# Softmax times values in plain float32, two heads side by side in TensorE's columns

## The chip, the core and the metric

The kernel runs on one core of one Trainium2 chip. The metric is device microseconds of the whole program: a median of 1966.94 over three runs (1965.1 to 1971.12). Engines are named as in the profile: PE is the matrix engine's matmuls, PEld its weight loads, DVE the vector engine, ACT the scalar engine, SP the queue that issues the DMAs. TensorE is granted its full 2.4 GHz in nearly the whole run (mean 0.996 of it).

## The reference, cut to what matters

Two transformer layers (MLA attention, neighbourhood attention, gated merge, MLP) run on 256 latent and 256 context tokens, then an mLSTM mixer and a windowed attention with a sink. In every attention, probabilities meet values:

```python
p = jax.nn.softmax(s, axis=-1).astype(v.dtype)
return jnp.einsum("bhqk,bkhe->bqhe", p, v)     # all float32, head dimension e = 64
```

MLA and neighbourhood attention have 8 heads per layer, the last attention 16 query heads. Layer 0 does this for the context tokens (256 keys) and the latent ones (512 keys), layer 1 and the last attention for the latent ones alone.

## The kernel before

Everything is computed with features or tokens on 128 partitions. Float32 products are made in three matmuls of the one-pass type `float32r`: each operand is stored as a rounded high part and a remainder (`split`, lines 728 to 734: ACT casts the high part, DVE subtracts to get the low one), and `mm3` (736) adds high·high, high·low and low·high. The class `HL` (663) holds such pairs.

An attention works by pairs of heads. `softmax_t` (1079) takes the scores of 128 queries in PSUM, makes the probabilities, transposes them on PE in blocks of 128 into PSUM, and splits the result into `pt`: one tile per head, with high and low part, up to 4 blocks of keys (`kt` = 4, or 2 for context queries) and 256 queries. `pv_mm` (1128) then multiplies values and `pt`: the values are the stationary operand, 256 queries stream. For head 1 of the pair the stationary operand is 128 columns wide (the 64 columns left of the head's come along), so its result lies in PSUM rows 64 to 127; head 0 then overwrites rows 0 to 63 with 64 columns. For `kt` = 4 that is 2 heads x 4 blocks x 3 = 24 matmuls, for `kt` = 2 it is 12. The values are split too: `vt0` and `vt` for neighbourhood attention, `mv` for MLA, `vt` and `v0` in `attn`. There are 32 such products: 16 in layer 0 (8 pairs, `kt` 2 and 4), 8 in layer 1, 8 in the last attention.

`pair_scores` (1111) is the place that already shares the array: two heads' scores contract over 64 rows each, in its upper and lower half, in turn, as one group.

All engine instructions are recorded first. `Recorder.flush` (336) then lists them by a planner with an own cost for each operation (`cost`, 287), 20 passes, free of the order in which the code is written; the lists are the engines' program order. `group` and `close` (184 to 201) make of several matmuls one operation that nothing is put between; its cost is the sum of the matmuls' times a share, plus 0.1. `either` lets the planner choose between ACT and DVE for one operation. Work of all stages shares 16 buffers of the tag `s8` (weights, `HL` pairs, `pt`). DVE also carries a background product over the modulation weights (`junk`), ACT and DVE split each weight chunk (`w`).

Of the kernel before, what the change touches and what calls it, by code (L numbers as in the profile page):

```python
# [6 lines left out]
F32 = mybir.dt.float32  # L7
# [127 lines left out]
class Recorder:  # L135
# [53 lines left out]
    def close(self):  # L189
        op, calls = self.open, self.calls  # L190
        self.open = None

        def run():
            for fn, a, k in calls:
                r = fn(*a, **k)  # L195
            return r

        op.fn, op.a, op.k = run, (), {}
        op.dur = op.dur * self.share + 0.1
        op.deps.discard(op.idx)  # L200
        self.ops.append(op)
# [472 lines left out]
class Kernel:  # L674
# [403 lines left out]

    def softmax_t(self, score, nk, pt, q0, bias=None, sink=None):

        nc, v = self.nc, self.nc.vector
        if callable(score):
            s = self.psum("S")
            p = self.t2()
            nc.hold(p)
            score(s[:, :nk])
        else:
            s, p = score
        if bias is not None:
            v.tensor_tensor(s[:, bias[0]], s[:, bias[0]], bias[1], ALU.add)  # L1090
        nm, ss = self.small(1), self.small(1)
        v.tensor_reduce(nm, s[:, :nk], AX.X, ALU.max, negate=True)
        if sink is not None:
            v.tensor_tensor(nm, nm, sink[0], ALU.min)
        nc.scalar.activation(p[:, :nk], s[:, :nk], AF.Exp, bias=nm, accum_out=ss)
        if sink is not None:
            es = self.small(1)
            nc.scalar.activation(es, nm, AF.Exp, bias=sink[1])
            v.tensor_tensor(ss, ss, es, ALU.add)
        v.reciprocal(ss, ss)  # L1100
        nc.either(lambda e: e.vector.tensor_scalar(p[:, :nk], p[:, :nk], ss, None, ALU.mult),
                  lambda e: e.scalar.activation(p[:, :nk], p[:, :nk], AF.Copy, scale=ss))
        tp = self.psum("T")
        nc.hold(pt)
        kt = nk // P
        for k in range(kt):
            nc.tensor.transpose(tp[:, k * P:(k + 1) * P], p[:, k * P:(k + 1) * P], self.cs("ident"))
        tv = tp[:, :nk].rearrange("p (k q) -> p k q", k=kt)
        self.split(tv, pt[:, 0, :kt, q0:q0 + P], pt[:, 1, :kt, q0:q0 + P])

# [14 lines left out]
    def new_pt(self):  # L1125
        return self.sb.tile([P, 2, 4, 256], F32R, tag="s8", name="pt")

    def pv_mm(self, ps, vt, vcols, pts, kt, first=None):


        def lhs(wh, k, e):
            c0, c1 = vcols
            if e == 0:
                return vt.ap(wh, k, slice(c0, c0 + 64))
            if c1 + k + wh == 0:
                return first
            f = (wh * vt.per + k) * vt.width + c1
            return vt.t[0].rearrange("p a k c -> p (a k c)")[:, f - 64:f + 64]

        for e in (1, 0):  # L1140
            for k in range(kt):
                self.mm3(ps[:128 if e else 64, :256], tuple(lhs(wh, k, e) for wh in (0, 1)),
                         (pts[e][:, 0, k, :], pts[e][:, 1, k, :]), k == 0, k == kt - 1)


    def block1(self, l, x, streams):
# [50 lines left out]
        kr = self.sb.tile([P, 4, 32], F32, tag="kr", name="kr")  # L1197
        vt0 = HL(self, 4, 256, per=4)

        def consume_v(j, ps):  # L1200
            self.split(ps[:, :256], vt0.ap(0, j), vt0.ap(1, j))
            nc.scalar.copy(kr[:, j], ps[:, 256:])
# [4 lines left out]
        nc.sync.dma_start(self.rw, self.i["rw"][l:l + 1].to_broadcast([P, NRW]))  # L1207
        qa, ka, mv = [], [], []
        for hf in range(2):
            ka_ = self.sb.tile([P, 4, 4, 96], F32, tag="tm", name="tm")  # L1210
            mv_ = HL(self, 4, 256, per=4)

            def consume_kv(j, ps, ka_=ka_, mv_=mv_):
                pv = ps.rearrange("p (h e) -> p h e", h=4)
                nc.scalar.activation(ka_[:, j, :, 0:64], pv[:, :, 0:64], AF.Copy, scale=rk[:, j:j + 1])
                hi = mv_.ap(0, j).rearrange("p (h e) -> p h e", h=4)
                lo = mv_.ap(1, j).rearrange("p (h e) -> p h e", h=4)
                self.split_scaled(pv[:, :, 64:128], rk[:, j:j + 1], hi, lo)

# [3 lines left out]
            ka.append(ka_)  # L1223
            mv.append(mv_)
            qa_ = self.sb.tile([P, nq, 4, 96], F32, tag="tm", name="tm")
# [21 lines left out]
        for pair in range(4):  # L1247
            pts = {}
            for e in range(2):
# [11 lines left out]
                for gi, toks, kt, cs in groups:  # L1261
                    pt = pts[gi, e] = self.new_pt()
                    for qi, j in enumerate(toks):
                        qs = slice(toksq.index(j) * P, toksq.index(j) * P + P)

                        def score(s, kt_=kt_, qt_=qt_, qs=qs, kt=kt):
                            n = kt * P
                            self.mm3(s, (qt_[:96, 0, qs], qt_[:96, 1, qs]), (kt_[:96, 0, :n], kt_[:96, 1, :n]),
                                     True, True)

                        self.softmax_t(score, kt * P, pt, qi * P)
            for gi, toks, kt, cs in groups:
                c = pair % 2 * P
                self.head_out(mv[pair // 2], (c, c + 64), [pts[gi, e] for e in range(2)], kt, y_mla, pair, csr(cs))
        if self.stage == 3:
# [5 lines left out]
        na = []  # L1281
        for hf in range(2):
            c0 = OFF_NA + hf * 256
            vt = HL(self, 4, 256, per=4) if hf else vt0
            if hf:
                self.tm_linear2(w_in, 0, c0 + 1024, h, range(4),
                                lambda j, ps, vt=vt: self.split(ps, vt.t[0][:, 0, j:j + 2], vt.t[0][:, 1, j:j + 2]))
            na.append([vt])
        for hf in range(2):
# [7 lines left out]
            rk_, rq_ = (self.tm_rstd(t.rearrange("p j h d -> p (j h) d")) for t in (k_, q_))  # L1297
            na[hf] = (q_, k_, na[hf][0], rq_, rk_)
        self.mark(f"b1.{l}.naat")
        for hf in range(2):  # L1300
            q_, k_, vt, rq_, rk_ = na[hf]
            for pair in range(2):
# [3 lines left out]
                for gi, toks, kt, cs in groups:  # L1306
                    pts = [self.new_pt() for _ in range(2)]
                    for qi, j in enumerate(toks):
                        qo = toksq.index(j) * P
                        sc = self.pair_scores(qt_, kt_, slice(qo, qo + P), kt * P)  # L1310
                        for e in range(2):
                            self.softmax_t(sc[e], kt * P, pts[e], qi * P,
                                           bias=(LAT, biases[e][:, qi, :]) if gi == 1 else None)
                    self.head_out(vt, (pair * P, pair * P + 64), pts, kt, y_na, hf * 2 + pair, csr(cs), True)
        if self.stage == 4:
# [77 lines left out]

    def head_out(self, vt, vcols, pts, kt, y, pair, cs, flip=False):
        ps = self.psum("T")
        self.pv_mm(ps, vt, vcols, pts, kt)
        d = lambda ap: ap.rearrange("p (j q) -> p j q", j=2)
# [338 lines left out]
    def attn(self, x):  # L1736
# [9 lines left out]
        k_ = self.sb.tile([P, 4, 4, 64], F32, tag="tm", name="tm")  # L1746
        vt = HL(self, 4, 256, per=4)
        v0 = self.sb.tile([P, P], F32R, tag="mk", name="v0")
        flat = lambda t: t.rearrange("p h d -> p (h d)")
# [9 lines left out]
        def keys(_):  # L1759
            self.mark(f"at.kv")  # L1760
            self.tm_linear2(w, 0, 1024, h, (2, 3, 0, 1), lambda j, ps: nc.scalar.copy(two(k_, j), ps))
            self.tm_linear2(w, 0, 1280, h, (2, 3, 0, 1),
                            lambda j, ps: self.split(ps, vt.t[0][:, 0, j:j + 2], vt.t[0][:, 1, j:j + 2]))
            nc.scalar.copy(v0.rearrange("p (o d) -> p o d", o=2),
                           vt.ap(0, 0, slice(0, 64)).rearrange("p (o d) -> p o d", o=1).to_broadcast([P, 2, 64]))
            self.tm_rms(k_.rearrange("p j h d -> p (j h) d"), self.rws("at_k"))
# [28 lines left out]
        def heads(hf):  # L1795
# [3 lines left out]
            for pair in range(2):  # L1799
                pts = [self.new_pt() for _ in range(2)]  # L1800
                qt_ = self.paired(q_, range(2), pair, 0.125)
                for qi in range(2):
# [3 lines left out]
                    for e in range(2):  # L1806
                        hd = hf * 4 + pair * 2 + e
                        self.softmax_t(sc[e], 512, pts[e], qi * P, bias=(far, tri),
                                       sink=(nsink[:, hd:hd + 1], sink[:, hd:hd + 1]))
                ps = self.psum("T")  # L1810
                self.pv_mm(ps, vt, (hf * 64, hf * 64), pts, 4, v0)
                m = hf * 2 + pair
# [151 lines left out]
```

## Time and profile before

| | before |
|---|---|
| runs, median (lowest to highest) | 1966.94 us (1965.1 to 1971.12) |
| the profiled execution's own time, its span | 1966.36 us, 1964.6 us |
| PE busy, PEld busy | 1925.8 us (98%), 1701.3 us (87%) |
| DVE busy, ACT busy | 1625.1 us (83%), 931.5 us (47%) |
| chain that ended last | PE 92%, DVE 5%, DMA 2%, ACT 1% |

PE counts as busy from a matmul's start to its modelled end, and matmuls overlap: what one costs in a stream is the distance from start to start, which the timeline gives as (length of a run minus one matmul's own duration) over (count minus one). A matmul of plain float32 leaves two records, each with its own load. Line 356 is the recorder's replay, so groups are told apart by tiles and shapes; line 195 is `close`, so matmuls of a group stand there.

### The profile page before, as it was taken

The page shows a single profiled execution, that of the slowest core. Times are in us where ns is not written, and L with a number is a line of the kernel's source. Part 1 is how long each engine was busy: PE and PEld are TensorE (multiplying, and loading weights), DVE is VectorE, ACT ScalarE, POOL GpSimd, SP SyncE. Part 2 cuts the span into 40 slices and gives each one's busy share as a digit, 9 for nine tenths or more (in the row PEclk, how much of TensorE's full clock was granted, in tenths as well). Part 3 has the DMA queues.
Part 4 walks back from the last instruction along what each step waited for, and adds up shares of the span by engine and source line. Part 5 has one row for each costly group of instructions (what it writes and reads, how often), then busy time and mean ns, then how long its engine had stood idle before and what let it go on. Part 6 is the DMA issues. An engine that isn't in the chain of part 4 may idle for free.

```text
span 1964.6 us, 30787 instructions
## 1 busy us (share of the span) xinstructions
PE 1925.8 (98%) x11692; PEld 1701.3 (87%) x11692; DVE 1625.1 (83%) x3393; ACT 931.5 (47%) x1684; POOL 0.2 (0%) x4
## 2 busy tenths in 40 slices
PE   7999999999999999999999899989999999999998
PEld 4899978889888888898999899987888888888997
DVE  8999898889887768999998888888848466577999
ACT  3467554344232333455674554546434335244565
POOL 0000000000000000000000000000000000000000
PEclk9999999999999999999999999999999999999999
DMA  8521513673567656353437577776474336243321
GB/s 288 179 67 42 156 44 98 224 236 108 182 222 230 224 195 192 98 167 79 112 109 227 154 238 257 260 194 138 101 121 78 91 81 121 41 130 98 95 65 34
DMA packets 196102, 283.67 MB, mean 144 GB/s; under 512 B 29281, under 2 KB 131169, under 8 KB 195825
## 3 DMA queue, kind: packets, MB, share of 16 engines
q1 hardware_dynamic: 195952, 281.69, 50.8%
q8 instruction: 92, 1.51, 0.3%
q14 instruction: 58, 0.47, 0.1%
HBM read 280.57 MB, written 1.08 MB: 143 GB/s over the span
## 4 chain that ended last, share of the span: by engine, by line
PE 92%; DVE 5%; DMA 2%; ACT 1%; issue 0%; SPq 0%; DVEq 0%; ACTq 0%
PE ps L356 90%; PE ps L195 1%; DMA raw<-in_ml_w_in_dram 1%; DVE sm L356 1%; DVE t L356 1%; DVE w L356 1%; DVE x L356 1%; DMA x<-in_xT_dram 0%; ACT t L356 0%; DVE tm L356 0%; ACT w L356 0%; DMA raw<-in_w_ff_dram 0%; DVE gt L356 0%; ACT gt L356 0%; DVE pt L356 0%
## 5 line engine op out<-in xcount | busy, mean ns | idle before, releaser
L356 PE MATMUL ps<-hl,w 128*128 128x512 f32 (+1 forms) x7272 | 1318.1, 340 | 3.7 <-DVE hl L356 2.0
L356 PEld LDWEIGHTS ps<-hl,w 128*128 128x128 f32 x7272 | 1129.1, 190 | 155.4 <-issue 6.5
L356 ACT CAST w<-raw 128x1024 fp32r<-128x1024 f32 (+2 forms) x367 | 378.3, 1039 | 500.0 <-PE ps L356 314.3
L356 DVE TENSOR_TENSOR w<-raw,w 128x1024 fp32r<-128x1024 f32 (+1 forms) x367 | 439.9, 1209 | 145.5 <-ACT w L356 142.3
L356 PE MATMUL ps<-w,hl 128*128 128x256 f32 (+3 forms) x2136 | 349.9, 317 | 0.9 <-DVE w L356 0.9
L356 PEld LDWEIGHTS ps<-w,hl 128*128 128x128 f32 x2136 | 312.5, 191 | 24.3 <-issue 1.8
L356 DVE SCALAR_TENSOR_TENSOR junk<-araw,cbc 128x1024 bf16<-128x1024 f32 x216 | 263.7, 1221 | 26.7 <-DMA araw<-in_ada_dram 24.7
L356 PE MATMUL ps<-cst,t 128*128 128x128 f32 (+2 forms) x600 | 94.8, 273 | 11.9 <-DVE t L356 9.4
L356 ACT ACTIVATE t<-ps,sm 128x512 f32<-128x512 f32 (+1 forms) x128 | 80.9, 635 | 50.8 <-DVE sm L356 50.1
L356 DVE SCALAR_TENSOR_TENSOR x<-ps,mod,x 128x256 f32<-128x256 f32 x192 | 81.5, 477 | 18.0 <-PE ps L356 17.2
L356 PEld LDWEIGHTS ps<-cst,t 128*128 128x128 f32 (+2 forms) x600 | 70.4, 141 | 28.0 <-DVE t L356 7.8
L356 PE MATMUL ps<-pt,hl 128*128 128x256 f32 (+1 forms) x668 | 92.7, 284 | 0.8 <-ACT t L356 0.4
L356 ACT ACTIVATE t<-ps 128x512 f32<-128x512 f32 (+1 forms) x116 | 56.7, 504 | 70.0 <-PE ps L356 68.9
L356 ACT CAST pt<-ps 128x512 fp32r<-128x512 f32 (+1 forms) x128 | 67.0, 534 | 48.1 <-PE ps L356 47.1
L356 DVE TENSOR_REDUCE sm<-ps 128x1 f32<-128x512 f32 (+3 forms) x146 | 86.2, 605 | 3.4 <-PE ps L195 2.1
L356 PEld LDWEIGHTS ps<-pt,hl 128*128 128x128 f32 (+1 forms) x668 | 81.6, 162 | 4.4 <-issue 1.5
L356 DVE TENSOR_TENSOR pt<-ps,pt 128x512 fp32r<-128x512 f32 (+1 forms) x128 | 78.0, 616 | 7.2 <-ACT pt L356 6.9
L356 DVE TENSOR_TENSOR t<-t,t 128x512 f32<-128x512 f32 (+1 forms) x76 | 44.6, 591 | 19.5 <-ACT t L356 18.2
L356 DVE TENSOR_TENSOR hl<-ps,hl 128x256 fp32r<-128x256 f32 (+1 forms) x64 | 33.1, 534 | 32.9 <-ACT hl L356 32.7
L356 ACT CAST hl<-ps 128x256 fp32r<-128x256 f32 (+1 forms) x64 | 28.5, 466 | 46.8 <-PE ps L356 46.7
L356 ACT ACTIVATE t<-x 128x512 f32<-128x512 f32 (+1 forms) x55 | 27.8, 540 | 40.7 <-DVE x L356 34.4
L356 ACT ACTIVATE hl<-t,mod 128x256 fp32r<-128x256 f32 x72 | 32.2, 502 | 25.6 <-DVE t L356 23.2
(134 smaller groups left out, 1406.0 us busy)
## 6 DMA issues: line engine op xcount, KB each, us to landing
araw<-in_ada_dram SPq DMA_DIRECT2D x128, 512.0 KB, 4.5
raw<-in_w_ff_dram SPq DMA_DIRECT2D x128, 512.0 KB, 4.6
raw<-in_ml_w_in_dram SPq DMA_DIRECT2D x72, 512.0 KB, 5.6
raw<-in_w_in_dram SPq DMA_DIRECT2D x68, 512.0 KB, 4.5
raw<-in_at_w_in_dram SPq DMA_DIRECT2D x20, 512.0 KB, 4.5
raw<-in_w_out_dram SPq DMA_DIRECT2D x16, 512.0 KB, 4.6
raw<-in_ml_w_out_dram SPq DMA_DIRECT2D x16, 512.0 KB, 5.4
raw<-in_w_uq_dram SPq DMA_DIRECT2D x12, 384.0 KB, 3.7
```

The source lines that it names most:

```text
L195: r = fn(*a, **k)
L356: r = run.fn(*run.a, **run.k)
```

## The change

`pt` becomes one plain float32 tile for both heads of a pair. After the transposes there is one copy out of PSUM, on ACT or DVE as the planner likes, in place of cast and subtraction. The values are kept as plain float32 (`nv`, `mv`, `vt`), written by one ACT copy or scaled copy. `pv_mm` is one group of float32 matmuls: for each block of keys head 0 into PSUM rows 0 to 63 and head 1 into rows 64 to 127, each with 64 stationary columns, so in the left and right half of the array's columns. The group's fixed cost in the planner goes from 0.1 to 0.4, for `pair_scores` too. `v0` goes.

```diff
-        op.dur = op.dur * self.share + 0.1
+        op.dur = op.dur * self.share + 0.4
...
-        self.split(tv, pt[:, 0, :kt, q0:q0 + P], pt[:, 1, :kt, q0:q0 + P])
+        dst = pt[:, e, :kt, q0:q0 + P]
+        nc.either(lambda r: r.scalar.copy(dst, tv), lambda r: r.vector.tensor_copy(dst, tv))
...
-        return self.sb.tile([P, 2, 4, 256], F32R, tag="s8", name="pt")
+        return self.sb.tile([P, 2, 4, 256], F32, tag="s8", name="pt")
...
-        for e in (1, 0):
-            for k in range(kt):
-                self.mm3(ps[:128 if e else 64, :256], tuple(lhs(wh, k, e) for wh in (0, 1)),
-                         (pts[e][:, 0, k, :], pts[e][:, 1, k, :]), k == 0, k == kt - 1)
+        nc.group(0.5)
+        for k in range(kt):
+            for e in range(2):
+                nc.tensor.matmul(ps[64 * e:64 * e + 64, :256], vt[:, k, vcols[e]:vcols[e] + 64], pt[:, e, k],
+                                 start=k == 0, stop=k == kt - 1)
+        nc.close()
...
-            self.split(ps[:, :256], vt0.ap(0, j), vt0.ap(1, j))
+            nc.scalar.copy(nv[:, j, :256], ps[:, :256])
...
-                self.split_scaled(pv[:, :, 64:128], rk[:, j:j + 1], hi, lo)
+                nc.scalar.activation(mv[:, j, hf * 256:hf * 256 + 256].rearrange("p (h e) -> p h e", h=4),
+                                     pv[:, :, 64:128], AF.Copy, scale=rk[:, j:j + 1])
...
-                            lambda j, ps: self.split(ps, vt.t[0][:, 0, j:j + 2], vt.t[0][:, 1, j:j + 2]))
-            nc.scalar.copy(v0.rearrange("p (o d) -> p o d", o=2),
-                           vt.ap(0, 0, slice(0, 64)).rearrange("p (o d) -> p o d", o=1).to_broadcast([P, 2, 64]))
+            self.tm_linear2(w, 0, 1280, h, (2, 3, 0, 1), lambda j, ps: nc.scalar.copy(vt[:, j:j + 2], ps))
```

On PE, the last two pairs of heads of the last attention, before (`hl` beside `pt` is a split value tile, `cst,t` a transpose of probabilities, `hl,w` the output projection):

```order
L356 MATMUL ps<-pt,hl 128x256
L356 MATMUL ps<-hl,w 128x256 x11
L356 MATMUL ps<-cst,t_3444 128x128 x4
L356 MATMUL ps<-pt,hl 128x256 x5
L356 MATMUL ps<-hl,w 128x256
L356 MATMUL ps<-pt,hl 128x256 x6
L356 MATMUL ps<-pt,hl 64x256
L356 MATMUL ps<-cst,t_3442 128x128 x4
L356 MATMUL ps<-cst,t_3456 128x128 x4
L356 MATMUL ps<-pt,hl 64x256 x11
```

The same place on PE now (`pt,vt` is the new product; the row says nothing of the column half):

```order
L356 MATMUL ps<-cst,t_3390 128x128 x4
L356 MATMUL ps<-cst,t_3388 128x128 x4
L356 MATMUL ps<-cst,t_3407 128x128 x4
L356 MATMUL ps<-cst,t_3405 128x128 x4
L356 MATMUL ps<-cst,t_3417 128x128 x4
L356 MATMUL ps<-cst,t_3419 128x128 x4
L195 MATMUL ps<-pt,vt 64x256 x8
L356 MATMUL ps<-hl,w 128x256
L195 MATMUL ps<-pt,vt 64x256 x8
L356 MATMUL ps<-hl,w 128x256 x48
```

Twenty-four matmuls of a pair, among which others stood, became eight in one piece, behind six softmaxes' transposes in a row.

On DVE, the same place before (`pt<-ps,pt` is the subtraction after a transpose):

```order
L356 TENSOR_SCALAR t_3442<-t_3442,sm 128x512
L356 TENSOR_SCALAR t_3456<-t_3456,sm 128x512
L356 TENSOR_TENSOR pt<-ps,pt 128x4x128
L356 TENSOR_TENSOR sm<-sm 128x1
L356 SCALAR_TENSOR_TENSOR x<-ps,mod_73,x 128x256
L356 RECIPROCAL sm<-sm 128x1
L356 TENSOR_TENSOR pt<-ps,pt 128x4x128 x2
L356 SCALAR_TENSOR_TENSOR x<-ps,mod_73,x 128x256
```

And on ACT now, where five of the last six copies of `pt` stand (the sixth is on DVE):

```order
L356 ACTIVATE t_3417,sm<-ps,sm 128x512
L356 ACTIVATE sm<-sm,rw 128x1
L356 ACTIVATE t_3419,sm<-ps,sm 128x512
L356 ACTIVATE sm<-sm,rw 128x1
L356 ACTIVATE t_3407<-t_3407,sm 128x512
L356 ACTIVATE t_3419<-t_3419,sm 128x512
L356 COPY pt<-ps 128x4x128 x5
L356 ACTIVATE hl<-t_3400 128x256
```

The subtractions left DVE's list; the copies queue on ACT, behind the scaling of the last probabilities. Over the program the 128 casts and 128 subtractions of `pt` become 111 copies on ACT (83 of 512, 28 of 256 columns) and 17 on DVE (13 and 4).

## Rows read from the trace of the kernel before

**Rows 1.** The page, busy time of each engine and the chain that ended last.
```profile
PE 1925.8 (98%) x11692; PEld 1701.3 (87%) x11692; DVE 1625.1 (83%) x3393; ACT 931.5 (47%) x1684; POOL 0.2 (0%) x4
...
PE 92%; DVE 5%; DMA 2%; ACT 1%; issue 0%; SPq 0%; DVEq 0%; ACTq 0%
```

**Rows 2.** Windows: stretch, length, busy time of PE, PEld, DVE, ACT, POOL; clock, DMA.
```profile
139.00:330.00 191.00, 191.00 (x1365) 170.68 (x1364) 174.20 (x430) 115.54 (x270) 0.00 (x0) 1.00 0.29 77
885.00:1040.00 155.00, 152.26 (x1189) 143.54 (x1189) 146.12 (x356) 98.42 (x192) 0.00 (x0) 0.98 0.42 109
1864.00:1917.95 53.95, 53.95 (x442) 50.25 (x440) 52.00 (x171) 35.88 (x83) 0.00 (x0) 1.00 0.19 60
1917.95:1945.24 27.29, 24.57 (x177) 19.23 (x176) 27.29 (x91) 21.90 (x57) 0.00 (x0) 1.00 0.06 20
```

**Rows 3.** Chain that ended last, window 1917 to 1946, shares by line.
```profile
by line: DVE sm L356 32.3%; DVE pt L356 18.5%; DVE x L356 10.7%; DVE t L356 9.1%; DVE ps L356 8.9%; DVE w L356 7.8%; DVE kq L356 4.3%; PE ps L195 3.2%; PE ps L356 3.0%; DVE hl L356 2.3%; issue 0.7%
```

**Rows 4.** Groups by form, softmax times values: busy us, mean ns | idle before.
```profile
L356 PE MATMUL ps<-pt,hl 128*128 128x256 f32 x332 | 50.5, 287 | 0.8 <-ACT t L356 0.4 <-DVE pt L356 0.3
L356 PE MATMUL ps<-pt,hl 128*64 128x256 f32 x336 | 47.2, 281 | 0.0
...
L356 PEld LDWEIGHTS ps<-pt,hl 128*64 128x64 f32 x336 | 39.5, 135 | 1.4 <-issue 1.1
```

**Rows 5.** Timeline of PE, runs of that product: start us, us, instructions.
```profile
914.28 1.24 PE L356 MATMUL ps<-pt,hl 128*128 128x256 f32 x9
...
917.10 1.17 PE L356 MATMUL ps<-pt,hl 128*64 128x256 f32 x8
```

**Rows 6.** Timeline of PE, the plain float32 matmuls of line 898.
```profile
17.03 3.61 PE L356 MATMUL ps<-raw,ct 128*2 128x256 f32 x16
```

**Rows 7.** Groups by form, the same matmuls and the 512-column stream.
```profile
L356 PE MATMUL ps<-hl,w 128*128 128x512 f32 x3768 | 881.2, 392 | 1.2 <-ACT hl L356 1.2
...
L356 PE MATMUL ps<-raw,ct 128*2 128x256 f32 x64 | 14.8, 379 | 0.0
```

**Rows 8.** Timeline of PE around one group of `pair_scores`.
```profile
286.06 1.85 PE L356 MATMUL ps<-hl,w 128*128 128x512 f32 x7
287.84 0.97 PE L195 MATMUL ps<-kq 64*128 64x512 f32 x6
288.74 1.43 PE L356 MATMUL ps<-hl,w 128*128 128x512 f32 x5
290.00 0.38 PE L356 MATMUL ps<-cst,t 128*128 128x128 f32 x2
```

**Rows 9.** Timeline of PEld over the same stretch.
```profile
286.15 1.34 PEld L356 LDWEIGHTS ps<-hl,w 128*128 128x128 f32 x6
287.84 0.53 PEld L195 LDWEIGHTS ps<-kq 64*128 64x128 f32 x6 [0.35 <-ACT t L356]
```

**Rows 10.** Groups by form, the splits on DVE and ACT that the change touches.
```profile
L356 DVE TENSOR_TENSOR pt<-ps,pt 128x512 fp32r<-128x512 f32 x96 | 65.0, 683 | 5.3 <-ACT pt L356 5.0
...
L356 ACT CAST pt<-ps 128x512 fp32r<-128x512 f32 x96 | 55.5, 588 | 37.9 <-PE ps L356 37.0
...
L356 DVE TENSOR_TENSOR hl<-ps,hl 128x512 fp32r<-128x512 f32 x28 | 18.6, 685 | 28.6 <-ACT hl L356 28.6
...
L356 DVE TENSOR_TENSOR hl<-ps,hl 128x256 fp32r<-128x256 f32 x36 | 14.5, 417 | 4.3 <-ACT hl L356 4.1
...
L356 DVE TENSOR_TENSOR pt<-ps,pt 128x256 fp32r<-128x256 f32 x32 | 13.2, 415 | 1.9 <-ACT pt L356 1.9
...
L356 ACT CAST pt<-ps 128x256 fp32r<-128x256 f32 x32 | 11.6, 372 | 10.2 <-PE ps L356 10.1
...
L356 DVE SCALAR_TENSOR_TENSOR hl<-ps,sm,hl 128x256 fp32r<-128x256 f32 x16 | 7.5, 478 | 0.0
```

More of the change, by code (lines that the diff above doesn't have):

```diff
@@ L1076, in rope, with softmax_t @@
             self.tt(*args)
-    def softmax_t(self, score, nk, pt, q0, bias=None, sink=None):
+    def softmax_t(self, score, nk, pt, e, q0, bias=None, sink=None):
         nc, v = self.nc, self.nc.vector
@@ L1125, in new_pt, with pv_mm @@
     def new_pt(self):
-        return self.sb.tile([P, 2, 4, 256], F32R, tag="s8", name="pt")
[L1128 to L1138, printed above, removed]
-        for e in (1, 0):
-            for k in range(kt):
-                self.mm3(ps[:128 if e else 64, :256], tuple(lhs(wh, k, e) for wh in (0, 1)),
-                         (pts[e][:, 0, k, :], pts[e][:, 1, k, :]), k == 0, k == kt - 1)
+        return self.sb.tile([P, 2, 4, 256], F32, tag="s8", name="pt")
+    def pv_mm(self, ps, vt, vcols, pt, kt):
+        nc = self.nc
+        nc.group(0.5)
[4 more added lines that the diff above has]
+        nc.close()
     def block1(self, l, x, streams):
@@ L1197, in block1 @@
         kr = self.sb.tile([P, 4, 32], F32, tag="kr", name="kr")
-        vt0 = HL(self, 4, 256, per=4)
+        nv = self.sb.tile([P, 4, 512], F32, tag="s8", name="nv")
         def consume_v(j, ps):
-            self.split(ps[:, :256], vt0.ap(0, j), vt0.ap(1, j))
+            nc.scalar.copy(nv[:, j, :256], ps[:, :256])
             nc.scalar.copy(kr[:, j], ps[:, 256:])
@@ L1207, in block1, with consume_kv @@
         nc.sync.dma_start(self.rw, self.i["rw"][l:l + 1].to_broadcast([P, NRW]))
-        qa, ka, mv = [], [], []
+        qa, ka = [], []
+        mv = self.sb.tile([P, 4, 512], F32, tag="s8", name="mv")
         for hf in range(2):
             ka_ = self.sb.tile([P, 4, 4, 96], F32, tag="tm", name="tm")
-            mv_ = HL(self, 4, 256, per=4)
-            def consume_kv(j, ps, ka_=ka_, mv_=mv_):
+            def consume_kv(j, ps, ka_=ka_, hf=hf):
                 pv = ps.rearrange("p (h e) -> p h e", h=4)
                 nc.scalar.activation(ka_[:, j, :, 0:64], pv[:, :, 0:64], AF.Copy, scale=rk[:, j:j + 1])
-                hi = mv_.ap(0, j).rearrange("p (h e) -> p h e", h=4)
-                lo = mv_.ap(1, j).rearrange("p (h e) -> p h e", h=4)
-                self.split_scaled(pv[:, :, 64:128], rk[:, j:j + 1], hi, lo)
+                nc.scalar.activation(mv[:, j, hf * 256:hf * 256 + 256].rearrange("p (h e) -> p h e", h=4),
+                                     pv[:, :, 64:128], AF.Copy, scale=rk[:, j:j + 1])
             self.tm_linear(self.i["w_ukv"][l], 0, 2, hf * 512, 512, ckv, range(4), consume_kv)
@@ L1223, in block1 @@
             ka.append(ka_)
-            mv.append(mv_)
             qa_ = self.sb.tile([P, nq, 4, 96], F32, tag="tm", name="tm")
@@ L1261, in block1 @@
                 for gi, toks, kt, cs in groups:
-                    pt = pts[gi, e] = self.new_pt()
+                    if not e:
+                        pts[gi] = self.new_pt()
                     for qi, j in enumerate(toks):
@@ L1269, in score @@
                                      True, True)
-                        self.softmax_t(score, kt * P, pt, qi * P)
+                        self.softmax_t(score, kt * P, pts[gi], e, qi * P)
             for gi, toks, kt, cs in groups:
-                c = pair % 2 * P
-                self.head_out(mv[pair // 2], (c, c + 64), [pts[gi, e] for e in range(2)], kt, y_mla, pair, csr(cs))
+                self.head_out(mv, (pair * P, pair * P + 64), pts[gi], kt, y_mla, pair, csr(cs))
         if self.stage == 3:
@@ L1281, in block1 @@
         na = []
[L1282 to L1288, printed above, removed]
+        self.tm_linear2(w_in, 0, OFF_NA + 1280, h, range(4), lambda j, ps: nc.scalar.copy(nv[:, j:j + 2, 256:], ps))
         for hf in range(2):
@@ L1297, in block1 @@
             rk_, rq_ = (self.tm_rstd(t.rearrange("p j h d -> p (j h) d")) for t in (k_, q_))
-            na[hf] = (q_, k_, na[hf][0], rq_, rk_)
+            na.append((q_, k_, rq_, rk_))
         self.mark(f"b1.{l}.naat")
         for hf in range(2):
-            q_, k_, vt, rq_, rk_ = na[hf]
+            q_, k_, rq_, rk_ = na[hf]
             for pair in range(2):
@@ L1306, in block1 @@
                 for gi, toks, kt, cs in groups:
-                    pts = [self.new_pt() for _ in range(2)]
+                    pt = self.new_pt()
                     for qi, j in enumerate(toks):
@@ L1311, in block1 @@
                         for e in range(2):
-                            self.softmax_t(sc[e], kt * P, pts[e], qi * P,
+                            self.softmax_t(sc[e], kt * P, pt, e, qi * P,
                                            bias=(LAT, biases[e][:, qi, :]) if gi == 1 else None)
-                    self.head_out(vt, (pair * P, pair * P + 64), pts, kt, y_na, hf * 2 + pair, csr(cs), True)
+                    c = hf * 256 + pair * P
+                    self.head_out(nv, (c, c + 64), pt, kt, y_na, hf * 2 + pair, csr(cs), True)
         if self.stage == 4:
@@ L1392, in residual, with head_out @@
         return consume
-    def head_out(self, vt, vcols, pts, kt, y, pair, cs, flip=False):
+    def head_out(self, vt, vcols, pt, kt, y, pair, cs, flip=False):
         ps = self.psum("T")
-        self.pv_mm(ps, vt, vcols, pts, kt)
+        self.pv_mm(ps, vt, vcols, pt, kt)
         d = lambda ap: ap.rearrange("p (j q) -> p j q", j=2)
@@ L1746, in attn @@
         k_ = self.sb.tile([P, 4, 4, 64], F32, tag="tm", name="tm")
-        vt = HL(self, 4, 256, per=4)
-        v0 = self.sb.tile([P, P], F32R, tag="mk", name="v0")
+        vt = self.sb.tile([P, 4, 256], F32, tag="s8", name="vt")
         flat = lambda t: t.rearrange("p h d -> p (h d)")
@@ L1761, in keys @@
             self.tm_linear2(w, 0, 1024, h, (2, 3, 0, 1), lambda j, ps: nc.scalar.copy(two(k_, j), ps))
-            self.tm_linear2(w, 0, 1280, h, (2, 3, 0, 1),
-                            lambda j, ps: self.split(ps, vt.t[0][:, 0, j:j + 2], vt.t[0][:, 1, j:j + 2]))
-            nc.scalar.copy(v0.rearrange("p (o d) -> p o d", o=2),
-                           vt.ap(0, 0, slice(0, 64)).rearrange("p (o d) -> p o d", o=1).to_broadcast([P, 2, 64]))
+            self.tm_linear2(w, 0, 1280, h, (2, 3, 0, 1), lambda j, ps: nc.scalar.copy(vt[:, j:j + 2], ps))
             self.tm_rms(k_.rearrange("p j h d -> p (j h) d"), self.rws("at_k"))
@@ L1799, in heads @@
             for pair in range(2):
-                pts = [self.new_pt() for _ in range(2)]
+                pt = self.new_pt()
                 qt_ = self.paired(q_, range(2), pair, 0.125)
@@ L1807, in heads @@
                         hd = hf * 4 + pair * 2 + e
-                        self.softmax_t(sc[e], 512, pts[e], qi * P, bias=(far, tri),
+                        self.softmax_t(sc[e], 512, pt, e, qi * P, bias=(far, tri),
                                        sink=(nsink[:, hd:hd + 1], sink[:, hd:hd + 1]))
                 ps = self.psum("T")
-                self.pv_mm(ps, vt, (hf * 64, hf * 64), pts, 4, v0)
+                self.pv_mm(ps, vt, (hf * 64, hf * 64), pt, 4)
                 m = hf * 2 + pair
```

## The prediction

> **What bounds the kernel now.** I read the page first. PE is busy 98% of the span and makes up 92% of the chain that ended last; DVE, at 83%, has 5% of that chain [rows 1]. The reader should see that DVE is busy and still seldom what is waited for. Then the windows, since the change lives only where there is attention: the two layers' attentions (139 to 330 us, 885 to 1040 us) and the last one (1864 to 1945 us). In the first, PE is busy 191.00 of 191.00 us beside DVE's 174.20, and so it is in 1864 to 1917.95, with 53.95 of 53.95 [rows 2]. There a microsecond taken from PE's stream is a microsecond of the end, and one taken from DVE is nothing. One stretch is different: from 1917.95 to 1945.24 us DVE is busy 27.29 of 27.29 us and PE 24.57 [rows 2], and the chain runs through DVE, 18.5% of it in the subtractions that make the low part of the probabilities [rows 3]. So I price PE's stream over the whole program, and DVE only in this last stretch.
>
> **What the old product costs PE.** 32 products: 24 with four blocks of keys, 24 matmuls each, and 8 with two blocks, 12 each, make 672 (668 stand in two groups [rows 4], four more read `v0`). Their busy sum, 50.5 + 47.2 us, counts the overlapping ends, so it is only an upper end. From start to start a run of nine takes (1.24 - 0.28)/8 = 0.120 us and a run of eight (1.17 - 0.28)/7 = 0.127 us, the first of these lengthened by the transposes ahead of it [rows 5]. I take 0.120: 672 x 0.120 = 80.6 us. Head 1, whose stationary operand is twice as wide, costs hardly more than head 0 (287 and 281 ns a matmul [rows 4]): what counts is the 256 columns that stream.
>
> **What the new product costs PE.** 224 program matmuls (24 x 8 + 8 x 4). Plain float32 with 256 streamed columns stands in this trace at one place, line 898: 32 program matmuls there left 64 records, so two passes each [rows 7], and 16 records run (3.61 - 0.38)/15 = 0.215 us apart [rows 6]. So there are 448 passes of 0.215 us, 96.5 us if each waits for the one before. That is 15.9 us more than now. Everything hangs on whether the two column halves run beside each other, and no row shows a column half at position 64. The nearest row is the other way of sharing the array, by rows: a group of `pair_scores` holds six matmuls of 512 columns and the next stream starts 288.74 - 287.84 = 0.90 us after it began [rows 8], where six in sequence at 881.2/3768 = 0.234 us [rows 7] would need 1.40 us and three 0.70. So two halves do run together there, and I carry this over to columns.
>
> But the overlap is not perfect for float32. The list has head 0 and then head 1 for each block, and each matmul is two passes, so passes come as A A B B A A B B. If passes start in order and two of one half can't overlap, the first A is alone, then the second A runs with the first B, the second B with the next A, and the last B is alone: 16 passes need 9 times 0.215 us, 8 passes need 5. Sum: 24 x 1.94 + 8 x 1.08 = 55.2 us (48.1 if they paired perfectly, 96.5 if not at all).
>
> Added to that are the changes of the array's shape. The `pair_scores` group takes 0.90 where three would be 0.70, and the five matmuls behind it take 290.00 - 288.74 = 1.26 us where 5 x 0.234 is 1.17 [rows 7, 8]; the loads of the first pair start only with its own matmuls, 0.35 us after the loads before had ended [rows 9]. I take 0.30 us a group: 32 x 0.30 = 9.6 us. The lower end is none: head 0's 64-column matmuls before already follow the 128-column ones, and the only idle that PE shows ahead of them is 0.0 us [rows 4]. The Trainium skill, TensorEngine Tiling, section Key Properties, has a rule against this change: a change of tiling mode drains the engine. The row on the row halves agrees in kind, with its 0.2 to 0.3 us; the 64-column row doesn't show it. By the rule the 9.6 us stand, by that other row the sum would be 9.6 us lower. I keep 9.6.
>
> New product: 55.2 + 9.6 = 64.8 us, so PE's stream gets 15.8 us shorter.
>
> **DVE and ACT.** DVE loses 65.0 + 13.2 us of subtractions for `pt`, 7.5 us for `mv`, and for the other values 8 x 0.417 + 6 x 0.685 = 7.4 us: 93 us [rows 10]. It gains 17 copies, at most 13 x 0.683 + 4 x 0.415 = 10.5 us by the same rows, and a few scalings of probabilities that the planner moves over from ACT. ACT's copy reads and writes what its cast did, so I price it as the cast: 83 x 0.588 + 28 x 0.372 = 59 us in place of 67 [rows 10]. Nearly all of this lies beside a full PE and is worth nothing. It counts in the last stretch: DVE there has about 18.5% of 29 us = 5.4 us of subtractions on the chain [rows 3]; without them it would need some 22 us, as much as PE's 24.57 less its own saving. So PE's 27.29 - 24.57 = 2.7 us of idle go [rows 2]. What is late next there is ACT: the list shows five copies in a row behind the last scalings, 5 x 0.588 = 2.9 us, while PE has the second-last product's matmuls and some of the projection to do. Elsewhere DVE's relief can give nothing, since PE doesn't wait; I take 0.
>
> **Sum.** The profiled execution took 1966.36 us (0.6 under the median of the runs): 1966.4 - 15.8 - 2.7 = 1947.9. Forecast 1948 us, 1.0% faster. Its own range is 1937 (no cost for the changes of shape) to 1958 (half of the overlap lost to loads and a new order with a few waits); the planner lists everything anew, which I allow 5 us either way.
>
> **Rivals.**
> 1. *The column halves take turns* (slower). One mechanism, at the 32 products: the second half's pass starts only when the first half's is through. 96.5 - 80.6 = 15.9 us more, or 25.5 with the changes of shape; less 2.7 at the end: 1980 to 1989, 1984 taken. It decides from the point where fewer than 106 of 448 passes overlap: (80.6 + 2.7 - 9.6)/0.215 = 342 slots are what the old time pays for, and I count on 256. For it: the one float32 run in the trace is strictly in turn [rows 6], though in one and the same tile; against it: the row halves [rows 8]. 20%.
> 2. *The group waits for its copies* (no change). Eight matmuls can't be split, so all of them wait for the last copy of both heads, where single matmuls of other work stood between the old ones. If every group stalls PE for one ACT copy, 32 x 0.588 = 18.8 us, and the gain is gone: 1948 + 18.8 = 1967. For it: five copies in a row in the last list. Against it: the old product hardly waited for its splits (0.8 us idle in all [rows 4]), and the list has other matmuls ahead of most groups. 10%.
> 3. *Better pairing.* 48.1 us and no cost of changing shape: 80.6 - 48.1 = 32.5, with 5 at the end 1929. 8%.
> 4. *Loads can't hide.* If a load can't run beside a matmul on the same rows, each pass adds 0.135 us [rows 4]: 448 x 0.350 = 157 us, 1966 + 76 - 3 = 2040 us. Against it: in the full array the loads run beside matmuls on the same rows, six within 1.34 us [rows 9] during seven matmuls of 1.85 us [rows 8]. 2%. The Trainium skill, TensorE: Matmul & The Clock Gate, section The mechanism, states just this rule, that a load passes a running matmul only when their row groups differ, which column halves don't; this trace disagrees with it for the full array.
>
> **How the numbers follow.** 60% for the forecast, 20, 10, 8 and 2% for the rivals. 0.3% of the time, 6 us, is about what a measurement of this kernel tells from no change, so faster means under 1961 and slower over 1973. Faster: nearly all of the 60, the 8, and some of the 10 where fewer groups wait, 69%. Slower: the 20 and the 2, 22%. Within: 9%. The range runs from 1930, just above the third rival, to 1984, the middle of the first: left out are half of the first, half of the third, and the fourth, some 16%.
>
> **What would show it.** In the timeline after, 16 records of one product should start 9 x 0.215 = 1.94 us before the next stream, with pairs of starts a few ns apart; records 0.215 us apart, 3.4 us for 16, mean rival 1. A gap ahead of the groups released by ACT or DVE `pt` means rival 2. DVE's busy time should fall to about 1545 us, and in the last 30 us DVE should no longer be busy throughout. I am wrong if the halves take turns, or if PE's chain grows waits on `pt` worth more than 10 us.

## The result and the profile after

The changed kernel takes 1935.91 us (1935.28 to 1936.93, four runs) against 1966.59 (the kernel before, with a fourth run): 0.9841 of the time, with a 95% interval of 0.9824 to 0.9858, so 31 us or 1.6% faster. The forecast was 1948 us; the measured time lies in the stated range, 1.1 us under the forecast's own.

The page after, engines and chain:

```profile
span 1935.0 us, 30174 instructions
PE 1904.0 (98%) x11468; PEld 1652.4 (85%) x11468; DVE 1565.0 (81%) x3264; ACT 917.7 (47%) x1654; POOL 0.2 (0%) x4
...
PE 94%; DVE 2%; DMA 2%; ACT 1%; issue 0%; SPq 0%; DVEq 0%; ACTq 0%
```

Beside [rows 1], PE is busy 21.8 us less and idle 7.8 us less (1935.0 - 1904.0 = 31.0 us; before 1964.6 - 1925.8 = 38.8). The share of PE didn't fall, because the program got shorter with it: a bound engine's gain shows in its busy time, not in its share. DVE lost 60 us of busy time and is on the chain for 2% in place of 5%.

The new product in the groups by form (busy us, mean ns | idle before), where [rows 4] had 97.7 us for 668 matmuls, and the new copies:

```profile
L356 ACT COPY pt<-ps 128x512 f32<-128x512 f32 x83 | 47.6, 590 | 18.8 <-PE ps L356 18.3
...
L195 PE MATMUL ps<-pt,mv 128*64 128x256 f32 x160 | 19.9, 387 | 0.0
L195 PE MATMUL ps<-pt,nv 128*64 128x256 f32 x160 | 19.9, 387 | 0.0
...
L195 PE MATMUL ps<-pt,vt 128*64 128x256 f32 x128 | 15.6, 385 | 0.0
...
L356 ACT COPY pt<-ps 128x256 f32<-128x256 f32 x28 | 10.0, 374 | 9.8 <-PE ps L356 9.4
L356 DVE COPY pt<-ps 128x512 f32<-128x512 f32 x13 | 8.9, 684 | 0.2
```

448 passes, as counted, and no idle ahead of any of them: the groups don't wait for their copies. One product of four key blocks in PE's timeline, between a group of scores and transposes, and the loads of that stretch:

```profile
276.03 0.62 PE L195 MATMUL ps<-kq 64*128 64x256 f32 x6
276.58 1.95 PE L195 MATMUL ps<-pt,nv 128*64 128x256 f32 x16
278.46 0.66 PE L356 MATMUL ps<-cst,t 128*128 128x128 f32 x4
```

```profile
276.58 1.49 PEld L195 LDWEIGHTS ps<-pt,nv 128*64 128x64 f32 x16
```

From its first start to the next stream it takes 278.46 - 276.58 = 1.88 us. In the records the sixteen starts come as eight pairs 7 ns apart, the pairs 0.216 us apart (0.267 between the first two): 8 x 0.216 = 1.73, and 0.15 us more, which I put down to changing the array's shape. All 24 such products take 1.88 us and the eight of two key blocks 1.01. So the column halves run side by side, and in 8 slots, not 9.

The end, where DVE had been busy throughout ([rows 2], 1917.95 to 1945.24), in PE's timeline after:

```profile
1918.81 2.56 PE L356 MATMUL ps<-cst,t 128*128 128x128 f32 x22
1921.31 1.95 PE L195 MATMUL ps<-pt,vt 128*64 128x256 f32 x16
1923.19 0.38 PE L356 MATMUL ps<-hl,w 128*128 128x256 f32 x1
1923.50 1.95 PE L195 MATMUL ps<-pt,vt 128*64 128x256 f32 x16
1925.38 6.02 PE L356 MATMUL ps<-hl,w 128*128 128x256 f32 x48
```

No row carries an idle time: PE goes through the last two pairs without a gap, the five queued copies on ACT included.

### The profile page after: what moved, and what is told of

Same layout as the page of the kernel before. It is cut to its first block, busy times and chain, and to the rows that moved or that the text cites. A ratio compares the mean times of both kernels' runs of the same rounds, so it can differ in the third digit from the quotient of the medians.

```text
span 1935.0 us, 30174 instructions
## 1 busy us (share of the span) xinstructions
PE 1904.0 (98%) x11468; PEld 1652.4 (85%) x11468; DVE 1565.0 (81%) x3264; ACT 917.7 (47%) x1654; POOL 0.2 (0%) x4
## 4 chain that ended last, share of the span: by engine, by line
PE 94%; DVE 2%; DMA 2%; ACT 1%; issue 0%; SPq 0%; DVEq 0%; ACTq 0%
PE ps L356 90%; PE ps L195 4%; DMA raw<-in_ml_w_in_dram 1%; DVE t L356 1%; DMA x<-in_xT_dram 0%; DVE junk L356 0%; DVE w L356 0%; DVE x L356 0%; DMA raw<-in_w_ff_dram 0%; DVE gt L356 0%; ACT gt L356 0%; ACT w L356 0%; ACT t L356 0%; DVE sm L356 0%; ACT hl L356 0%
## 5 line engine op out<-in xcount | busy, mean ns | idle before, releaser
L356 ACT COPY pt<-ps 128x512 f32<-128x512 f32 (+1 forms) x111 | 57.5, 535 | 28.6 <-PE ps L356 27.7
L356 DVE TENSOR_TENSOR t<-t,t 128x512 f32<-128x512 f32 (+1 forms) x76 | 44.7, 591 | 21.8 <-ACT t L356 20.4
L356 DVE TENSOR_TENSOR hl<-ps,hl 128x256 fp32r<-128x256 f32 (+1 forms) x50 | 26.1, 535 | 28.0 <-ACT hl L356 28.0
L356 DVE TENSOR_SCALAR t<-t,sm 128x512 f32<-128x512 f32 (+1 forms) x104 | 45.8, 447 | 1.7
L356 ACT CAST hl<-t 128x256 fp32r<-128x256 f32 (+1 forms) x76 | 37.0, 506 | 15.9 <-DVE t L356 12.9
L356 DVE TENSOR_TENSOR hl<-t,hl 128x256 fp32r<-128x256 f32 (+1 forms) x76 | 40.3, 548 | 4.6 <-ACT hl L356 3.3
L356 DVE TENSOR_TENSOR t<-t 128x256 f32<-128x256 f32 (+1 forms) x63 | 32.5, 528 | 9.0 <-ACT t L356 8.6
```

What stands on the lines that cost most here:

```text
L356: r = run.fn(*run.a, **run.k)
```

## The experiments

Each ran beside the kernel before, which took 1966.95 us beside the first four and 1967.14 us beside the other three (the relief alone, and the planner's constant at 0.4 before and at 0.2).

**The changed kernel again.**

> The changed kernel once more, beside the experiments on the same chip: about 1936 us. Its products are measured from start to start: 16 records of four key blocks should again need 1.88 us to the next stream, 8 records 1.01 us.

1934.59 us, ratio 0.9840 (0.9824 to 0.9857), with the same 1.88 and 1.01 us. This is the base for the others: 1934.6 to 1935.9.

**Heads in turn.**

```diff
-        for k in range(kt):
-            for e in range(2):
+        for e in range(2):
+            for k in range(kt):
                 nc.tensor.matmul(ps[64 * e:64 * e + 64, :256], ...
```

> The product with the loops swapped: all key blocks of head 0, then all of head 1, so that matmuls of different column halves no longer alternate. Everything else, also the planner's cost, is as in the changed kernel. Theory A (passes start in the order of the list and only neighbours in different halves overlap): 16 passes need 15 slots of 0.216 us instead of 8, 8 passes need 7 instead of 4, so 24 x 7 x 0.216 + 8 x 3 x 0.216 = 41 us more, about 1977 us, slower than before the change. Theory B (each half has a queue of its own and the two run beside each other whatever the order): unchanged, about 1936 us.

1954.80 us, ratio 0.9938 (0.9923 to 0.9953): 19 to 20 us more, half of what theory A says, and not nothing, as theory B has it. PE's timeline, a product with four key blocks and one with two:

```profile
977.16 2.86 PE L195 MATMUL ps<-pt,nv 128*64 128x256 f32 x16
979.96 0.77 PE L356 MATMUL ps<-cst,t 128*128 128x128 f32 x5
```

```profile
152.66 1.09 PE L195 MATMUL ps<-pt,mv 128*64 128x256 f32 x8
153.69 0.61 PE L356 MATMUL ps<-kq 96*128 96x256 f32 x2
```

Sixteen passes now take 2.80 us, eight still 1.03. The records don't name the half; I tell the heads apart by their passes' spacing of 0.216 us. In the records of the first, head 0's passes start alone at 977.16, .43, .65 and .86, and head 1's first pass starts at 978.08 together with head 0's fifth, ahead of the sixth, seventh and eighth, which stand before it in the list. From there four pairs follow, and head 1's last four go alone. All 24 products of four key blocks have this pattern, so it is no late copy of head 1 that makes it. So passes of different halves are not held in the list's order, but the starts fit one that is started early only when it stands about four places behind the pass whose turn it is: with four passes a head all pair up, with eight the first four go alone. Both theories are wrong as they stood. 24 x (2.80 - 1.88) = 22 us is the price, 19 to 20 were measured. It also shows that the overlap of halves is what the product's gain rests on.

**DVE's pass put back.**

```diff
-        nc.either(lambda r: r.scalar.copy(dst, tv), lambda r: r.vector.tensor_copy(dst, tv))
+        nc.scalar.copy(dst, tv)
+        v.tensor_tensor(dst, tv, dst, ALU.max)
```

> After each copy of transposed probabilities, which ACT now always makes, DVE takes the larger of the PSUM values and the copy into the copy, which changes nothing in the values and costs DVE what the old subtraction did, in the same place between ACT and PE: DVE back to about 1640 us busy. Theory A (the gain is PE's shorter product, DVE's relief is worth what PE no longer waits, 4 us): 1938 to 1943 us. Theory B (a large part of the gain is DVE's relief): 1950 us or more, with PE idle before transposes or products.

1951.45 us, ratio 0.9921 (0.9906 to 0.9936): 15.5 to 17 us of the gain are gone, though PE's product is as short as in the changed kernel. By its number this is theory B. The page:

```profile
span 1949.1 us, 30276 instructions
PE 1906.2 (98%) x11468; PEld 1654.1 (85%) x11468; DVE 1607.8 (82%) x3360; ACT 932.4 (48%) x1686; POOL 0.2 (0%) x4
...
PE 88%; DVE 7%; DMA 2%; ACT 2%; issue 1%; SPq 0%; DVEq 0%; ACTq 0%
```

PE's busy time is 2.2 us over the changed kernel's, its idle time 1949.1 - 1906.2 = 42.9 us against 31.0. To find where the time goes, I compare the two executions by the number of the matmul in PE's list. This one is 0.4 us behind the changed kernel's at the matmul that starts there at 1785.1 us, 6.2 behind at 1797.1, 6.3 at 1880.1 and 14.0 at the last. So the loss falls in two places.

The first is the normalisation ahead of the last attention, before any of its softmaxes (`sm` holds its sums there). PE in this run:

```profile
1788.10 0.41 PE L356 MATMUL ps<-cst,t 128*128 128x128 f32 x2 [2.07 <-DVE sm L356]
1789.76 1.19 PE L356 MATMUL ps<-cst,sm 128*128 128x128 f32 x4 [1.25 <-DVE sm L356]
1792.27 0.79 PE L356 MATMUL ps<-w,hl 128*128 128x256 f32 x2 [1.32 <-ACT hl L356]
```

The same place in the changed kernel, with one wait:

```profile
1785.44 0.60 PE L356 MATMUL ps<-cst,sm 128*128 128x128 f32 x4
1787.26 0.41 PE L356 MATMUL ps<-cst,t 128*128 128x128 f32 x2 [1.21 <-DVE t L356]
```

The clock falls too: windows of this run, then of the changed kernel (columns as in [rows 2]):

```profile
1788.00:1793.00 5.00, 2.33 (x9) 1.86 (x10) 4.22 (x22) 1.29 (x4) 0.00 (x0) 0.56 0.06 21
```

```profile
1788.00:1793.00 5.00, 5.00 (x44) 5.00 (x43) 5.00 (x21) 3.11 (x7) 0.00 (x0) 1.00 0.00 0
```

A mean of 0.56 is mostly the lower of the clock's two levels, 1.2 of 2.4 GHz; PE had been busy 1.02 of the 3.00 us before. The four matmuls `cst,sm` take 1.19 us in place of 0.60. DVE does nothing on probabilities here, and the next run, which has no pass of DVE's on them at all, loses the same 5.8 us at the same place. So these 5.8 us are put down to the new list and not to the pass; what in the planner made them is open.

The second place is the last attention's softmaxes, 7.7 us from 1880.1 on. The chain that ended last, in this run from 1860 us to the end, and in the changed kernel from 1853 us:

```profile
by line: DVE sm L356 21.9%; DVE pt L356 13.6%; DVE t L356 11.2%; PE ps L356 9.8%; DVE x L356 6.7%; DVE w L356 5.1%; DVE ps L356 4.8%; ACT t L356 4.5%; DVE tm L356 4.5%; DVE kq L356 4.2%; PE ps L195 4.2%; DVE hl L356 2.2%; DVE zs L356 1.6%; 
```

```profile
by line: PE ps L356 62.8%; PE ps L195 30.1%; DVE x L356 3.4%; issue 0.0%
```

Here DVE is 76% of the chain, its pass 13.6%, and PE waits for it; without the pass the chain is PE's. In the two layers the pass costs next to nothing: 0.4 us in all at 1785.1. Without the 5.8 us of the list this run would stand near 1945.6 us (an estimate from the one profiled execution), between the two theories.

**DVE's relief alone.**

```diff
-        self.split(tv, pt[:, 0, :kt, q0:q0 + P], pt[:, 1, :kt, q0:q0 + P])
+        dst = pt[:, 0, :kt, q0:q0 + P]
+        nc.either(lambda r: r.scalar.copy(dst, tv), lambda r: r.vector.tensor_copy(dst, tv))
...
-                         (pts[e][:, 0, k, :], pts[e][:, 1, k, :]), k == 0, k == kt - 1)
+                         (pts[e][:, 0, k, :], pts[e][:, 0, k, :]), k == 0, k == kt - 1)
```

> The kernel before with its product of 672 float32r matmuls, but without the 128 subtractions that make the low part of the probabilities: each is one copy on ACT or DVE, and the product reads the high part in the low part's place (that part of the computation is left out, PE's work is the same). DVE falls by some 70 us, PE's stream stays. Theory A (PE bounds the kernel before; the relief of DVE is worth something only once PE's product is shorter): 1960 to 1966 us. Theory B (the two parts simply add up; putting a DVE pass back cost the changed kernel 15.5 us, so taking it away here gains as much): about 1951 us.

1964.45 us, ratio 0.9983 (0.9974 to 0.9993): 2.7 us. By its number this is theory A.

```profile
span 1964.9 us, 30661 instructions
PE 1927.6 (98%) x11692; PEld 1705.8 (87%) x11692; DVE 1577.6 (80%) x3294; ACT 918.7 (47%) x1655; POOL 0.2 (0%) x4
```

DVE is 47 us less busy than before, and the profiled spans are alike (1964.9 and 1964.6 us). But PE's waits at the start of the last attention are those of the run above:

```profile
1804.52 0.41 PE L356 MATMUL ps<-cst,t 128*128 128x128 f32 x2 [1.80 <-DVE sm L356]
1806.40 1.19 PE L356 MATMUL ps<-cst,sm 128*128 128x128 f32 x4 [1.47 <-DVE sm L356]
1808.91 0.79 PE L356 MATMUL ps<-w,hl 128*128 128x256 f32 x2 [1.32 <-ACT hl L356]
```

The kernel before has one wait there:

```profile
1805.46 0.41 PE L356 MATMUL ps<-cst,t 128*128 128x128 f32 x2 [1.21 <-DVE t L356]
```

The granted clock from 1806 to 1812 us was 0.50 here, with PE busy 2.12 of the 5.00 us before, and 1.00 in the kernel before. By the number of the matmul this execution is 1.1 us ahead of the kernel before at 1800.1 us, 4.7 behind at 1813.1, 4.9 at 1920.0 and 0.3 at the last matmul: the list costs 5.8 us, and the last stretch, where DVE made the chain before [rows 3], wins 4.6. Without the 5.8 this run would stand near 1958.7 us (again an estimate), below theory A's range and still well above theory B's 1951.

The four combinations as measured:

| | with DVE's pass on the probabilities | without |
|---|---|---|
| old product | 1967.1 | 1964.5 |
| new product | 1951.5 | 1934.6 to 1935.9 |

Alone the parts bring 15.5 and 2.7 us, 18 together; both at once bring 31 to 32. It looks as if 13 to 14 us were to be had only with both. But the two runs with one part alone each carry 5.8 us of their lists that neither the kernel before nor the changed one has. Without these (an estimate from one profiled execution of each) the parts bring 21.3 and 8.5 us, 30 together, and 1 to 3 us are left for an effect of both at once, no more than a new list moves by itself. (The new product's row is also without the splits of the values, some 15 us of DVE's time; the old product's row has them.)

**The planner's constant**, three times: 0.1 in the changed kernel, 0.4 in the kernel before, 0.2 in the changed kernel.

```diff
-        op.dur = op.dur * self.share + 0.4
+        op.dur = op.dur * self.share + 0.1
```

> The planner's fixed cost of a group back to 0.1, all else as in the changed kernel, so only the order of the lists differs. Theory A (the order matters only by a few waits): within 5 us of 1936. Theory B (the new constant, and so a better order, is a good part of the gain): 1943 us or more.

1940.18 us, ratio 0.9861 (0.9847 to 0.9876), 4 to 6 us slower than with 0.4.

> The kernel before with the planner's fixed cost of a group at 0.4 alone. Theory A (the order moves a few waits): within 5 us of 1966.9. Theory B (a better order through this constant is a part of the change's gain): 1960 us or less.

1967.27 us, ratio 1.0004 (0.9992 to 1.0016): nothing.

> The changed kernel with the planner's fixed cost at 0.2, which is nearer to what groups take in the trace: planned 1.93 us for a product that takes 1.88 to 1.97, and 0.88 for scores that take 0.90. Theory A (near the true cost the order changes little): 1932 to 1940 us. Theory B (a cost nearer to the measured one removes the waits that are left, some 6 us): 1930 us or less.

1937.22 us, ratio 0.9848 (0.9832 to 0.9864), within 1 to 3 us of 0.4, no better. The constant is worth at most some 5 us of the 31, and only with the new product. So theory A holds in all three, at 0.1 just so. These runs also show what a new list moves by itself: up to some 5 us.

## Why the prediction was right, and where not

*Direction and mechanism: right.* The column halves run beside each other, so rivals 1 and 4 are out, and rival 2 with them: no idle time stands before any of the new groups.

*The new product: mis-sized.* I put 55.2 us for the passes, from passes that start strictly in the list's order (9 slots). They take 8 slots, 4 for two key blocks: 24 x 8 x 0.216 + 8 x 4 x 0.216 = 48.3 us. This was the third rival's first half, to which I gave 8%. The heads-in-turn run shows why: the engine starts a pass of the other half ahead of its place. The price of a single pass, 0.215 us, was right within a nanosecond (0.216).

*Changes of shape: nearly right.* 0.30 us a group was taken; it is 0.15 within and behind each group and, by the starts ahead (mostly 0.33 us behind a 512-column matmul where 0.227 is usual, 0.21 behind a 256-column one for 0.120), about 0.09 in front, so 32 x 0.24 = 7.7 us for 9.6.

*The old product: nearly right.* 0.120 us a matmul was read from one run; from start to start, all 672 together give 82.7 us, 0.123 each, for the 80.6 used.

With these three PE's stream is shorter by 82.7 - 48.3 - 7.7 = 26.7 us, not 15.8. This is the term that the forecast had wrong, and most of why it came out 12 us too slow. (Its own lower end, the sum without the changes of shape, is 1947.9 - 9.6 = 1938.3 and not 1937.) PE's busy time fell by only 21.8 us: the other matmuls take 4.5 us more than before, from start to start, and why is open.

*DVE: nearly right, in part by luck.* I took 2.7 us for the last stretch and nothing elsewhere. At the same matmul of the stream `ps<-hl,w`, the one nine tenths through, between the layers and the last attention, the changed kernel is 18.2 us ahead (1716.4 us against 1734.6); from there to the last matmul it is 11.0 us faster (214.7 against 225.7). By the prices above the product accounts for 18.7 and 7.9 of these (0.98 us for four key blocks, 0.38 for two). So some 3 us are left for PE's waits in the last attention, and nothing before it. The layers agree only in sum: layer 0 gained 5.9 us for 10.9, which is open, layer 1 12.0 for 7.9. In layer 1 the kernel before had waits of 2.3 us at 888 to 892 us, and the clock at 0.62 from 890 to 896 us, after PE had been busy 3.27 of 5.00 us. The changed kernel's layer 1 has no such wait and a clock of 1.00 (860 to 945 us), so a part of the gain is the better list. The stretch in the kernel before:

```profile
890.00:896.00 6.00, 5.36 (x23) 4.66 (x24) 6.00 (x27) 1.71 (x5) 0.00 (x0) 0.62 0.41 109
```

What I did not price is that the short product needs DVE's relief in the last attention, where DVE was busy 52.00 of 53.95 us before [rows 2]: with its pass kept, DVE makes the chain there and 7.7 us are lost. What I wrote of the last stretch, that there DVE is as long as PE, is so with the short product from about 1860 us on. That the forecast of 18.5 us equals 15.5 + 2.7, what the two parts brought one by one, is chance, since both of these carry the 5.8 us of their lists.

*DVE's busy time:* I expected about 1545 us, it is 1565. The durations of all of DVE's instructions did fall by 75 us (1832 to 1757 us, summed from the records: 94 taken away, as worked out, and some 18 added); but the page's busy time counts overlapping instructions once, and two subtractions of 0.68 us take 1.27 us one behind the other. A busy time is to be forecast from such distances, as I had done for PE and not for DVE.

## What to carry to other kernels

When one engine bounds a stage and a second is nearly full beside it, price a change on both together: in the last attention here DVE's pass, kept, cost 7.7 us, about what PE's shorter product gains there (7.9). Test such a change in its four combinations, but where a planner lists everything anew for each, compare the executions matmul by matmul before a remainder is read as an effect of both parts: of 13 to 14 us here all but 1 to 3, by the estimate above, came from one place where two of the four lists left PE waiting and then at about half the clock. And where two halves of the array are shared, interleave their matmuls in the list: the same work cost 19 to 20 us more with the heads one after the other.

## What the runs showed of the hardware that was not expected

- Two column halves of TensorE ran plain float32 passes in pairs 7 ns apart, at 0.216 us a pair of 256 columns, so two cost what one did.
- A matmul was started before others that stand ahead of it in the list, when these waited for their own half of the array: head 1's first pass at 978.08 us, before head 0's sixth at 978.29. By the starts it looked about four places ahead. The Trainium skill, TensorE: Matmul & The Clock Gate, section The mechanism, says that matmuls start and end strictly in program order; this run differs, and the measurement decides.
- Loads of both halves ran beside the matmuls of both, 16 in 1.49 us, though they use the same rows of the array. The same section of the Trainium skill lets a load pass a running matmul only when their row groups differ, and, some lines above that, also when it goes to a background buffer for weights; here it passed with the same rows, and no run tells which buffer it went to.
- A change to column halves and back cost 0.24 us a group, 0.09 of it in front. The Trainium skill, TensorEngine Tiling, section Key Properties, says that a change of tiling mode drains the engine; the trace agrees in kind, with that price.
- In both runs with one part alone three waits ahead of the last attention (4.64 and 4.59 us in all, where the kernel before and the changed one wait 1.21) cost 5.8 us and not the 3.4 by which they are longer. The granted clock fell with them, to 0.56 from 1788 to 1793 us after PE had been busy 1.02 of 3.00 us, and to 0.50 from 1806 to 1812 us after 2.12 of 5.00 us.
